# A parallel-mixer decoder layer: the fifth head's division given its natural priority, the seventh head's products with its reciprocals moved to GpSimd

## The chip, the cores and the metric

The kernel runs on one core of a Trainium2 chip. The time is the device time of one execution in microseconds; the time before is the median of three runs. One further execution was taken with the hardware profiler, and all rows below come from it. The engines are called PE (TensorE; PEld is its weight load), DVE (VectorE), ACT (ScalarE), POOL (GpSimd) and SP (SyncE, which here only issues DMAs).

## The reference

One layer over 1024 tokens and 16 meta tokens with 1024 channels. The part around the change is the second of four mixers, causal attention with 8 heads:

```python
z = rms_norm(x) @ w_in                       # one projection for all branches
s = einsum(q, k) masked causally             # per head, 96 wide
o = softmax(s) @ v                           # per head, 64 wide
y_b = (o * silu(mg)) @ w_out_mla             # the heads side by side, gated, projected
m = sum_i sigmoid(g_i) * y_i                 # four mixers; the other three: pooling, two convolutions
x = x + rms_norm(m @ w_o)
```

The softmax is computed as exp(s - max) @ [v, 1]. Its denominator is thus one more row of the product, and the division by it is done afterwards, on the 64 rows of the head's output.

## The kernel before, in words

The kernel has three stages. The first, up to 638 us of the profiled span, is the input projection with the preparation of all branches. The second, from 638 to 838 us, is attention; PE fills its gaps there with the output projections of the three other mixers ("fills", matmuls into the tile ps_y). The third projects the attention's output (ps_u), sums up the mixers and multiplies by w_o.

Every operation is recorded first (`Plan.record`, L325) and put in order by a list scheduler in `Plan.flush` (L364): it walks through an estimated time, and each engine takes of its ready operations the one with the lowest `prio`. An operation's `prio` is its place in the recording minus `lift`; `plan.ahead(n)` (L263) raises `lift` by n, so a negative n puts operations behind some 450 later ones. A DMA's estimated landing has 4500 ns on top of its bytes, and `plan.slow(5000)` adds 5000 (L448, L449). What comes out is a fixed order for each engine; at run time an engine takes its instructions in that order and waits at semaphores. All instructions therefore carry L362, the line that issues them, in the profile, and are told apart by their tiles.

Attention runs over units (h, c): 8 heads, numbered from 0, by two halves of 512 tokens (`attend`, L1507). A unit works through tiles of 128 keys: scores on PE into ps_s (five banks), a mask added by DVE on the diagonal (maskT), exp on ACT to p, a rounded copy on ACT and a residual on POOL (pt; this "split" gives two terms of reduced precision for one of full precision), and the products with v on PE into the one bank ps_o. When a unit ends, ACT copies ps_o to ol (L1556); ol has two buffers, one per head. The row maxima of the next unit (mxs, mr, qt; DVE reading ps_s) go on beside it.

The division of a head, for h < 7, is `sums` (L1558) and `head_out` (L1584). Its steps, in order:

1. SP moves the row of denominators from ol into a 32 x 32 tile lc.
2. DVE takes the reciprocal of lc.
3. SP writes lc to DRAM (r), and then reads it back broadcast over 64 rows into rb (a single buffer).
4. For each half c, DVE multiplies ol by rb into op, 64 rows by 512 columns (L1589). The even head of a pair fills rows 0 to 63, the odd head rows 64 to 127.
5. After the odd head, POOL multiplies op by the gate smg, and ACT and POOL split the result into boM, the operand of the last projection.

An ol buffer is free again once both products of step 4 have read it. The last head (h = 7) takes its reciprocals through PE and multiplies from PSUM (`sums_pe`, L1569). A fill (`fills`, L1603) is six matmuls into one of two ps_y banks, followed on DVE by th<-th,ps_y (gate times projection) and m<-m,th (sum; some of them on POOL).

The loop that records all this sets the priority of the division:

```python
with plan.ahead(300 if h == H - 1 else -450):
    if h == H - 1:
        head_out(h, c, sums_pe(h, c))
    elif c:
        for k, rb in enumerate(sums(h)):
            head_out(h, k, rb)
```

Of the kernel before, what the change touches and what calls it, by code (L numbers as in the profile page):

```python
# [41 lines left out]
H = 8  # L42
# [429 lines left out]
def trunk_kernel(ctx, tc, a):  # L472
    nc = tc.nc
    plan = Plan(nc)
    PE, ACT, DVE, POOL, SP = (plan.engine(e) for e in ("PE", "ACT", "DVE", "POOL", "SP"))
# [7 lines left out]
    def ld(out, in_):  # L483
        SP.dma_start(f(out) if out.dtype == F32R else out, f(in_) if in_.dtype == F32R else in_)
# [10 lines left out]
    def mul(eng, out, x, y):  # L495
        eng.tensor_tensor(out, x, y, op=ALU.mult)

    def split(hi, lo, src, eng=None):
        copy(hi, src)
        sub(eng or POOL, lo, src, f(hi))  # L500
# [937 lines left out]
    def load_q(h, c):  # L1438
        qt[h, c] = qk.tile([NA, 2, 512], F32R, tag="q", bufs=3, name="qt")
        ld(qt[h, c][:QK].rearrange("p s n -> p (s n)"), q_dram[c][h].rearrange("p s n -> p (s n)"))  # L1440
        if h < FIRST:
            ld(f(qt[h, c])[QK:NA, 0], top_dram[:, c].rearrange("r a n -> r (a n)"))
# [18 lines left out]
    def load_k(h, n0, n1):  # L1461
        e = h % 2
        ld(kt[e][:64, :, n0:n1], k_dram[h // 2][64 * e:64 * (e + 1), :, n0:n1])

    def load_kv(h):
        e, k_, v_ = h % 2, kt[h % 2], vt[h % 2]
        k_ = k_[:, :, :L]
        if h < 2:
            k_rows(k_, h, lambda x: x)
        else:  # L1470
            load_k(h, CUT, L)
        if h == 1:
            return
        load_v(h)

    def load_v(h):
        v_ = vt[h % 2]
        v = v_dram[h // 4][h % 4]
        e = v[:NM, 1:9].rearrange("p (c j) d -> p c j d", j=4)[:, :, 3]
        for r, w in ((0, slice(0, P)), (32, slice(0, P)), (64, slice(P, 192))):  # L1480
            ld(vs[h % 2][r:r + NM, :, :w.stop - w.start], e[:, :, w])
        ld(v_[:, 0:8].rearrange("p j c -> p (j c)"), v[:, 0:8].rearrange("p j c -> p (j c)"))
# [22 lines left out]
    ol = {}  # L1505
# [52 lines left out]
    def sums(h):  # L1558

        lc = at.tile([32, 32], F32, tag="lc", bufs=2, name="lc")  # L1560
        rb = at.tile([64, 2, 512], F32, tag="rb", name="rb")
        with plan.slow(5000):
            ld(lc, ol[h][64:65].rearrange("p j (a n) -> p (j a) n", n=32))
            DVE.reciprocal(lc, lc)
            ld(r_dram[h].rearrange("(p n) -> p n", n=32), lc)
            ld(rb.rearrange("p j n -> p (j n)"), r_dram[h].partition_broadcast(64))
        return rb[:, 0], rb[:, 1]

    def sums_pe(h, c):  # L1569

        pc = bank("s")[:, :256].rearrange("p (j n) -> p j n", n=64)
        for j in range(4):
            PE.transpose(pc[:, j].in_order(), ol[h][64:, c, P * j:P * (j + 1)], ident[64:, 64:])
        lc = at.tile([P, 4], F32, tag="lcp", bufs=2, name="lcp")
        with plan.late(700):
            DVE.reciprocal(lc, pc[:, :, 0])
        rb = bank("s")[:64]
        for j in range(4):
            PE.transpose(rb[:, P * j:P * (j + 1)], lc[:, j:j + 1].to_broadcast([P, 64]), ident)
        return rb  # L1580

    op, smg = {}, {}

    def head_out(h, c, rb):  # L1584

        e = h % 2
        if e == 0:
            op[c] = at.tile([P, 512], F32, tag=f"op{c}", name="op")
        mul(DVE, op[c][64 * e:64 * (e + 1), :], ol[h][:64, c], rb)  # L1589
        if e:  # L1590
            mul(POOL, op[c], op[c], smg[h][:, 512 * c:512 * (c + 1)])
            b = boM[c][h // 2]
            split(b[:, 0], b[:, 1], op[c])
# [50 lines left out]
    def refill():  # L1644
        count["u"] += 1
        while count["f"] < min(48, 48 * count["u"] / (NUNIT - 2)):

            with plan.ahead(-400):
                next(fill, None)
            count["f"] += 1  # L1650
# [9 lines left out]
    def lead_to(i, n=0):  # L1660

        while lead["i"] <= min(i, len(seq) - 1) or lead["steps"] < n:
            if next(steps, "end") == "end":
                lead["steps"] = math.inf
            lead["steps"] += 1
# [5 lines left out]
    for i, (h, c) in enumerate(seq):  # L1671
        with plan.behind() if i else nullcontext():
            if i + 2 < len(seq):
                load_q(*seq[i + 2])
            if c == 0 and h + 1 < H:
                load_kv(h + 1)
                if i == 0:
                    with plan.behind():
                        load_v(1)
            if h % 2 and c == int(h < H - 1):  # L1680
                smg[h] = at.tile([P, NT], F32, tag="smg", name="smg")
                ld(smg[h], z_dram[f"mg{h // 2}"])
        for j, _ in enumerate(attend(h, c)):
            if c and j == 4 and h + 2 < H:
                load_k(h + 2, 0, CUT)
            units += 1
            lead_to(-1, min(5 + units * 10 / 14, 5 * (i + 3)))
            refill()
        lead_to(i + 1)

        with plan.ahead(300 if h == H - 1 else -450):
            if h == H - 1:
                head_out(h, c, sums_pe(h, c))
            elif c:
                for k, rb in enumerate(sums(h)):
                    head_out(h, k, rb)
# [247 lines left out]
```

## Time and profile before

| | us |
|---|---|
| median of 3 runs (lowest, highest) | 969.65 (969.29, 969.93) |
| profiled execution, whole time | 968.91 |
| profiled execution, span of its instructions | 967.1 |
| stage 1, 0 to 638: PE busy | 632.59 |
| stage 2, 638 to 838: PE, DVE, ACT, POOL busy | 197.89, 159.01, 115.04, 137.32 |
| stage 3, 838 to 967.1: PE busy | 119.96 |
| granted PE clock, mean | 0.997 |

The span runs from the first to the last instruction of the profiled execution; its whole time is 1.81 us longer. A row of a timeline in this document reads: start in us, duration in us (of several merged instructions where x is above 1), engine, line, operation, output tile <- input tiles, shapes, count, and in brackets how long the engine had been idle just before and what released it. A row of waits reads: engine, tile and line that waited <- what it waited for: us in total, times, longest. A PE that is busy is not one at its peak, since matmuls are pipelined and their ends are modelled. The time recorded for a POOL instruction is rough.

### The profile page before, as it was taken

Reading aid. Unit: us, or ns where it says so; the run is one execution under the profiler, and the core shown is the slowest. Engines: PE = TensorE matmul, PEld = TensorE weight load, DVE = VectorE, ACT = ScalarE, POOL = GpSimd, SP = SyncE. Lnnn points to the kernel's source line nnn. Section 1 sums busy time; section 2 is a strip of 40 time slices with the busy share of each in tenths; the row PEclk is TensorE's granted clock in tenths of the full one; section 3 lists DMA queues with packets and bytes.
Section 4 is the critical chain, followed back from the end, with each engine's and each line's share of the span. In section 5 each row is a group of like instructions: output and inputs, shape, how many; then the busy total and the mean of one; then the engine's idle time right before and its main releaser. Section 6 shows DMA issues by size and latency. Waiting matters only on the chain.

```text
span 967.1 us, 15247 instructions
## 1 busy us (share of the span) xinstructions
PE 950.4 (98%) x5003; PEld 808.9 (84%) x5003; DVE 696.0 (72%) x1113; ACT 449.1 (46%) x914; POOL 678.0 (70%) x628
## 2 busy tenths in 40 slices
PE   8999999999999999999999999999999999999996
PEld 7999899889888887888888878888888788788885
DVE  5856959988779855544536768346778889799757
ACT  7743233444344455554444344366555555225622
POOL 5957555666576787896679679655567786647955
PEclk9999999999999999999999999999999999999998
DMA  8145566668787687787655688699899664783633
GB/s 258 45 126 144 167 198 213 216 196 270 231 265 255 205 248 214 220 255 216 195 168 169 205 268 276 208 318 262 272 221 297 175 187 132 272 267 95 211 113 142
DMA packets 136330, 203.03 MB, mean 210 GB/s; under 512 B 19672, under 2 KB 83159, under 8 KB 135483
## 3 DMA queue, kind: packets, MB, share of 16 engines
q1 hardware_dynamic: 127274, 185.28, 63.3%
q10 hardware_dynamic: 8656, 15.74, 4.4%
q0 software_dynamic: 320, 1.05, 0.3%
q8 instruction: 39, 0.64, 0.3%
q14 instruction: 41, 0.33, 0.1%
HBM read 129.11 MB, written 72.88 MB: 209 GB/s over the span
## 4 chain that ended last, share of the span: by engine, by line
PE 90%; POOL 3%; DVE 2%; issue 2%; ACT 1%; DMA 1%; DVEq 0%; SPq 0%; POOLq 0%; ACTq 0%
PE ps_pa L362 16%; PE ps_pb L362 16%; PE ps_pc L362 15%; PE ps_o L362 9%; PE ps_y L362 8%; PE ps_s L362 8%; PE ps_pd L362 7%; PE ps_u L362 7%; PE ps_x L362 5%; POOL S L362 1%; POOL lsq L362 1%; ACT junk L362 1%; DVE c L362 0%; DMA lacc<-acc 0%; POOL u L362 0%
## 5 line engine op out<-in xcount | busy, mean ns | idle before, releaser
L362 PE MATMUL ps_pb<-T,S 128*128 128x512 f32 (+2 forms) x792 | 172.0, 359 | 0.0
L362 PE MATMUL ps_pa<-B,A 128*128 128x512 f32 (+2 forms) x792 | 171.7, 360 | 0.0
L362 POOL TENSOR_TENSOR A<-raw,A 128x512 fp32r<-128x512 f32 x84 | 114.3, 1368 | 61.3 <-ACT A L362 47.7
L362 PEld LDWEIGHTS ps_pb<-T,S 128*128 128x128 f32 x792 | 134.3, 189 | 22.4 <-issue 1.2
L362 PEld LDWEIGHTS ps_pa<-B,A 128*128 128x128 f32 x792 | 134.4, 188 | 22.3 <-issue 1.0
L362 POOL TENSOR_TENSOR S<-ss,S 128x512 fp32r<-128x512 f32 x84 | 116.0, 1393 | 51.8 <-ACT S L362 51.7
L362 POOL TENSOR_TENSOR pt<-p,pt 128x512 fp32r<-128x512 f32 (+1 forms) x96 | 102.8, 1094 | 52.5 <-PE ps_s L362 32.6
L362 DVE TENSOR_TENSOR u<-ps_pb,u 128x512 f32<-128x512 f32 (+2 forms) x66 | 40.3, 610 | 87.4 <-PE ps_pb L362 84.3
L362 DVE SCALAR_TENSOR_TENSOR ps_w<-conv,par,ps_w 128x512 f32<-128x512 f32 x116 | 87.1, 751 | 2.3
L362 PE MATMUL ps_y<-bo,whl 128*128 128x512 f32 x288 | 85.7, 403 | 0.9 <-DVE th L362 0.9
L362 PE MATMUL ps_pc<-B,S 128*128 128x512 f32 (+1 forms) x396 | 85.8, 358 | 0.0
L362 ACT ACTIVATE S<-ss 128x512 fp32r<-128x512 f32 x84 | 50.4, 627 | 74.5 <-DVE ss L362 43.7
L362 PE MATMUL ps_pd<-T,A 128*128 128x512 f32 (+2 forms) x396 | 84.9, 359 | 0.0
L362 PE MATMUL ps_pc<-T,S 128*128 128x512 f32 (+1 forms) x396 | 84.4, 359 | 0.0
L362 ACT ACTIVATE p<-ps_s 128x512 f32<-128x512 f32 (+4 forms) x112 | 49.7, 444 | 60.3 <-PE ps_s L362 29.2
L362 PEld LDWEIGHTS ps_pc<-T,S 128*128 128x128 f32 x396 | 66.8, 188 | 11.2 <-issue 0.7
L362 PEld LDWEIGHTS ps_pd<-T,A 128*128 128x128 f32 x396 | 67.1, 189 | 10.7
L362 PEld LDWEIGHTS ps_pc<-B,S 128*128 128x128 f32 x396 | 66.4, 189 | 10.2
L362 PE MATMUL ps_o<-pt,vt 128*128 128x512 f32 (+7 forms) x288 | 68.7, 346 | 0.2 <-ACT ol L362 0.2
L362 PE MATMUL ps_s<-qt,kt 100*128 100x512 f32 (+4 forms) x336 | 67.8, 324 | 0.0
L362 PEld LDWEIGHTS ps_s<-qt,kt 100*128 100x128 f32 (+1 forms) x336 | 54.1, 176 | 10.3 <-DVE qt L362 0.6
L362 ACT ACTIVATE A<-raw 128x512 fp32r<-128x512 f32 x84 | 52.0, 626 | 22.3 <-PE ps_pd L362 9.7
(281 smaller groups left out, 1890.4 us busy)
## 6 DMA issues: line engine op xcount, KB each, us to landing
raw<-in_w_in_dram SPq DMA_DIRECT2D x52, 512.0 KB
th<-th SPq DMA_DIRECT2D x32, 512.0 KB
th<-z ACTq DMA_DIRECT2D x60, 256.0 KB
v<-vhl SPq DMA_DIRECT2D x16, 384.0 KB
qt<-q SPq DMA_DIRECT2D x16, 384.0 KB
vt<-v SPq DMA_DIRECT2D x8, 768.0 KB
bo<-bo SPq DMA_DIRECT2D x6, 1024.0 KB
w_out_mla<-whl SPq DMA_DIRECT2D x16, 256.0 KB
```

What stands on the lines that cost most here:

```text
L362: getattr(self.handle[o["eng"]], o["op"])(*map(real, o["args"]), **{k: real(v) for k, v in o["kw"].items()})
```

## The change

Two conditions are added. In `head_out`, the two products ol x rb of h = 6 are issued on POOL and no longer on DVE; their operands and results stay. In the unit loop, all steps of the division of h = 4 are recorded with no lift, where they had a lift of -450. The other heads keep their engine and their priority. As the scheduler orders everything anew, other instructions can change places too.

```diff
@@ head_out @@
         e = h % 2
         if e == 0:
             op[c] = at.tile([P, 512], F32, tag=f"op{c}", name="op")
-        mul(DVE, op[c][64 * e:64 * (e + 1), :], ol[h][:64, c], rb)
+        mul(POOL if h == H - 2 else DVE, op[c][64 * e:64 * (e + 1), :], ol[h][:64, c], rb)
         if e:
             mul(POOL, op[c], op[c], smg[h][:, 512 * c:512 * (c + 1)])
@@ the unit loop @@
-        with plan.ahead(300 if h == H - 1 else -450):
+        with plan.ahead(300 if h == H - 1 else 0 if h == 4 else -450):
             if h == H - 1:
                 head_out(h, c, sums_pe(h, c))
```

## The prediction

> **What bounds the kernel now.** I read first the page's busy shares, then the busy time by stage, the waits of TensorE (PE) in the attention stage, and last the instructions of each engine, in order of time, around the two places that the edits touch.
>
> ```profile
> PE 950.4 (98%) x5003; PEld 808.9 (84%) x5003; DVE 696.0 (72%) x1113; ACT 449.1 (46%) x914; POOL 678.0 (70%) x628
> ```
> ```profile
> 638.00:838.00 200.00, 197.89 (x1059) 164.07 (x1058) 159.01 (x357) 115.04 (x264) 137.32 (x139) 1.00 0.80 232
> ```
> ```profile
> PE ps_s L362 <- ACT p L362: 1.0, 1, 1.0
> PE ps_y L362 <- DVE th L362: 0.9, 1, 0.9
> PE ps_o L362 <- ACT ol L362: 0.2, 1, 0.2
> ```
>
> The stage row gives start and end, length, then busy us (and instructions) of PE, PEld, DVE, ACT, POOL. PE is busy 197.89 of 200 us of attention: both edits lie in a stage with only 2.1 us of recorded PE idleness, and that total is these three waits, 1.0 + 0.9 + 0.2. An edit that takes no matmul away can win about that much here, and can lose more.
>
> The waits of 1.0 and 0.2 belong to the products of the fourth head (heads are counted from 0 in the code, so this is h = 3), which no edit touches:
>
> ```profile
> 767.02 2.68 DVE L362 TENSOR_TENSOR op<-ol,rb 64x512 f32<-64x512 f32 x2
> ...
> 769.74 0.42 PE L362 MATMUL ps_s<-kt,qt 96*128 96x328 f32 x1 [0.95 <-ACT p L362]
> 770.38 3.26 PE L362 MATMUL ps_o<-pt,vt 128*128 128x512 f32 x13 [0.22 <-ACT ol L362]
> ```
>
> The wait of 0.9 stands at the end of the stage, just behind the products of the seventh head (h = 6):
>
> ```profile
> 831.46 0.69 DVE L362 TENSOR_TENSOR m<-m,th 128x512 f32<-128x512 f32 x1
> 832.31 0.69 DVE L362 SCALAR_TENSOR_TENSOR th<-th,ps_y 128x512 f32<-128x512 f32 x1 [0.16 <-PE ps_y L362]
> 833.03 0.69 DVE L362 TENSOR_TENSOR m<-m,th 128x512 f32<-128x512 f32 x1
> 833.75 0.68 DVE L362 TENSOR_TENSOR op<-ol,ps_s 64x512 f32<-64x512 f32 x1
> 834.47 1.29 DVE L362 TENSOR_TENSOR op<-ol,rb 64x512 f32<-64x512 f32 x2
> 835.68 0.67 DVE L362 SCALAR_TENSOR_TENSOR th<-th,ps_y 128x512 f32<-128x512 f32 x1
> 836.39 1.05 DVE L362 TENSOR_TENSOR m<-m,th 128x512 f32<-128x512 f32 x1
> ```
> ```profile
> 836.41 1.67 PE L362 MATMUL ps_y<-bo,whl 128*128 128x512 f32 x6 [0.91 <-DVE th L362]
> ```
>
> VectorE (DVE) runs without a gap here. The pair op<-ol,rb at 834.47 is the h = 6 pair; behind it in DVE's queue stands the th that empties the PSUM bank for which PE waits 0.91 us.
>
> **Edit 1: the h = 6 products go to GpSimd (POOL).** It removes 1.29 us of DVE work ahead of the th of 835.68. It adds two instructions to POOL, whose row at that time is:
>
> ```profile
> 828.93 1.34 POOL L362 TENSOR_TENSOR boM<-op,boM 128x512 fp32r<-128x512 f32 x1 [0.51 <-ACT boM L362]
> 835.23 3.36 POOL L362 TENSOR_TENSOR op<-op,smg 128x512 f32<-128x512 f32 x2 [4.96 <-DVE op L362]
> ```
> ```profile
> L362 POOL TENSOR_TENSOR boM<-op,boM 128x512 fp32r<-128x512 f32 x6 | 7.8, 1302 | 0.6 <-ACT boM L362 0.5
> L362 POOL TENSOR_TENSOR op<-op,smg 128x512 f32<-128x512 f32 x8 | 12.4, 1563 | 5.0 <-DVE op L362 5.0
> ```
>
> POOL has no product of 64 rows, so I bound one by its instructions over 128 rows of the same 512 columns: 1.30 to 1.56 us. The lower end is nearer (the gap is otherwise quiet), so the two take 2.6 us. POOL stands idle for 4.96 us, 830.27 to 835.23, waiting for this very product; the pair fits, and the gates op<-op,smg behind it come no later. What would bite if that cover were gone is told under the rivals.
>
> The price lies on DVE. Its sums m<-m,th take 0.69 us while POOL idles (831.46, 833.03) and 1.05 while POOL works (836.39, inside the row of 835.23). With POOL now busy from 830.3 on, I charge both earlier sums 0.36 us. So the th at 835.68 moves by -1.29 + 2 x 0.36 = -0.57, and PE's wait shrinks from 0.91 to 0.34. Bounds: no charge at all gives -0.91 (PE has nothing more to win there); if each of the two sums waited out a whole POOL instruction, 2 x 1.30, the th comes 1.31 us later and PE loses that much. I take -0.57, by the rows of the same sum in the same place.
>
> A rule speaks against this edit. The Trainium skill, page "SBUF — State Buffer", section "Who interferes with whom", says that a VectorE instruction with two SBUF inputs and a GpSimd instruction that reads SBUF contend for a port pair that is held for the whole instruction, so that the later one stands still. The sums' 0.69 and 1.05 us agree with a wait of that kind that is only partly served out; by the rule's worst case the term would be +1.31 in place of -0.57, which is the rival "lock" below.
>
> Behind the stage, PE's first products ps_u want the last boM. With the pair done early, the gates are held by op<-ol,ps_s of h = 7 (833.75, done 834.43) and no longer by the pair's end near 835.76. So boM comes over a microsecond earlier, while PE comes at most 0.91 earlier; no new wait arises, and as none of PE's three waits lies there, none goes. I count 0.
>
> **Edit 2: the h = 4 division at its natural place.** The priority of all of its steps rises by 450 places: the DMA of the sums, the reciprocal, two more DMAs on SP, and two products. Their places now:
>
> ```profile
> 754.15 0.56 SPq L362 DMA_DIRECT2D lc<-ol  x1
> ...
> 766.99 0.38 SPq L362 DMA_DIRECT2D r<-lc  x1
> 771.41 0.46 SPq L362 DMA_DIRECT2D rb<-r  x1
> ...
> 822.27 0.46 SPq L362 DMA_DIRECT2D rb<-r  x1
> ```
> ```profile
> 789.54 1.70 DVE L362 TENSOR_TENSOR op<-ol,rb 64x512 f32<-64x512 f32 x1
> 791.55 1.38 DVE L362 TENSOR_TENSOR op<-ol,rb 64x512 f32<-64x512 f32 x1
> ```
>
> The three DMAs (754.15, 766.99, 771.41) are short issues of 0.38 to 0.56 us on SP; rb has a single buffer, which the h = 3 products hold until 769.70, so rb cannot come much before 771.41. Only the products can move far: from 789.54 to no earlier than about 775.8 (771.41 plus the 4.42 us that lie between r<-lc and the rb<-r behind it, as nearest row for a landing). The planner charges such a transfer some 10 us (4.5 + 5 and the bytes), so I place them near 782. Moved: 1.70 + 1.38 = 3.08 us of DVE from behind to ahead of the row maxima, mask adds and bank evacuations of 782 to 789. Queued behind them are PE's bank turnover and the qt rows of the next unit. PE shows no gap in this stretch (columns as in the stage row):
>
> ```profile
> 780.00:790.00 10.00, 10.00 (x53) 8.11 (x52) 8.82 (x21) 5.00 (x14) 7.35 (x9) 1.00 0.67 204
> ```
>
> Nothing can be won at the spot itself. What hides the move is DVE's 1.18 idle us of 780 to 790 and PE's filler matmuls. If that does not do, the row of its kind is h = 3, where such a pair cost 0.95 + 0.22 = 1.17 us; of the six pairs of h = 0 to 5 it is the only one with a PE wait beside it, since the stage has no PE wait but the three above. So 0 to +1.17; I take 0, by five of six.
>
> It also frees the ol buffer early. Now the copy of h = 6 waits for it, while PE works fillers:
>
> ```profile
> 792.97 0.60 ACT L362 ACTIVATE ol<-ps_o 128x512 f32<-128x512 f32 x1 [0.20 <-DVE op L362]
> ```
> ```profile
> 785.71 0.24 PE L362 MATMUL ps_o<-pz,vs 80*128 80x16 f32 x1
> ...
> 785.90 1.36 PE L362 MATMUL ps_y<-bo,whl 128*128 128x512 f32 x5
> 791.65 1.32 PE L362 MATMUL ps_y<-bo,whl 128*128 128x512 f32 x5
> 792.94 1.09 PE L362 MATMUL ps_y<-bo,whl 128*128 128x512 f32 x4
> ```
> ```profile
> 838.08 43.57 PE ps_u L362 x192
> ```
>
> The bank is complete at 785.95 and is copied out at 792.97. With ol free the copy moves some 6 us forward, and up to 14 fillers (at 43.57 / 192 = 0.227 us, 3.2 us) are put off. The number of matmuls stays, so PE's sum stays; the late fillers need DVE, 0.67 + 0.69 to 1.05 us for each six, against 6 x 0.227 = 1.36 of PE. That is 0 to 0.36 us per six, at most 0.8 for fourteen, under a DVE gap of 3.58 us ahead of 825.41:
>
> ```profile
> 825.41 0.69 DVE L362 SCALAR_TENSOR_TENSOR th<-th,ps_y 128x512 f32<-128x512 f32 x1 [3.58 <-PE ps_y L362]
> ```
>
> I take 0. **Sum:** -0.57 + 0 + 0 = -0.57. The profiled execution took 968.91 us (span 967.1 and 1.81 around it), so about 968.3; it lies 0.74 below the median of 969.65, to which I add the same step: 969.1.
>
> **The rivals.**
>
> *Stall at the new place.* The h = 4 pair makes PE wait as h = 3 does: -0.57 + 1.17 = +0.60, 970.3. For it: DVE is 88% busy there. Against: five of six pairs.
>
> *Lock.* Each sum beside a POOL product waits it out: +1.31, 971.0. For it: op<-ol,rb takes 1.70 and 1.38 beside a busy POOL and 0.65 without. Against: the sum at 836.39, beside POOL, takes only 1.05. With the stall as well it is +2.48, 972.1.
>
> *Slower: POOL's queue.* The planner's landing time for rb of h = 6 is a guess. If the products stand ahead of head 7's last residual splits, POOL waits in order:
>
> ```profile
> 821.23 3.94 POOL L362 TENSOR_TENSOR pt<-p,pt 128x512 fp32r<-128x512 f32 x4
> ```
> ```profile
> 836.92 0.63 ACT L362 ACTIVATE boM<-op 128x512 fp32r<-128x512 f32 x1 [7.42 <-POOL op L362]
> ```
>
> rb is issued at 822.27 and, by the 4.42 us above, there at 826.7; the splits would start at 826.7 + 2.6 = 829.3, 8.1 us late. The unit behind them, and with it op<-ol,ps_s of 833.75, ends 8.1 us later, at 842.5; gate, rounding and residual (1.30 + 0.63 + 1.30) give boM at 845.8, where PE asks for it at 837.92 + 22 x 0.227 = 842.9. PE loses 2.9 us, net +2.3: 972.0. It decides from a delay of the splits of 5.2 us on. Against: the planner's 10 us are more than the 4.42, so it would place the pair behind the splits.
>
> *Faster: both waits go.* Everything is ordered anew from the DMA of 754.15 on, so the waits at 769 may vanish with the one at 836: -2.1, 967.6. Against: the h = 3 products that cause them keep their priority.
>
> *No move.* The planner finds no earlier place for the h = 4 pair; edit 1 works alone: 969.1, as forecast.
>
> **How the numbers follow.** Forecast, with no move: 0.47. Stall 0.10, lock 0.06, both 0.05, POOL's queue 0.12, both waits gone 0.20. A difference under 0.2% (1.94 us) cannot be told from no change here. Faster, under 967.7: 0.20. Slower, over 971.6: 0.12 + 0.05 = 0.17. Within: 0.63. The range goes from 967.2, which takes in most of the fast case, to 971.2, which takes in stall and lock and leaves the 0.17 out.
>
> **What would show it.** Right: no op<-ol,rb on DVE between 825 and 838 and two on POOL near 1.3 us each ahead of the last gates; the wait ps_y <- DVE th at the end at 0.3 us, with the sums there near 1.05; the h = 4 pair near 782 and the copy of h = 6 near 786; PE waits of the stage near 1.5 us. Wrong: a PE wait of 1 us or more between 775 and 800, a POOL gap in front of its op<-ol,rb while pt is waiting, DVE sums near 2 us, or a stage that ends beyond 838.5 or before 836.5.

## The result and the profile after

| | before | after |
|---|---|---|
| median of 22 runs each, on the same chips, us | 969.93 | 968.57 |
| lowest to highest | 968.72 to 972.6 | 967.86 to 970.89 |
| ratio, with its 95% interval | | 0.9987 [0.9981, 0.9993] |
| profiled execution: span | 967.1 | 967.1 |
| attention in it, first ps_s to first ps_u | 638.11 to 837.92 = 199.81 | 639.39 to 838.38 = 198.99 |

By the ratio the changed kernel is faster by 0.13%, which is 1.26 us (0.68 to 1.84); the two medians differ by 1.36. That is inside the 0.2% that the prediction called no change, though this many runs can tell it from nothing. The forecast of 969.1 is 0.5 us too high.

The two profiled executions have the same span, because the one of after lost 1.28 us before attention began (639.39 against 638.11). PE has the same order of work up to there in both kernels, all 3407 of its recorded matmuls. The chain of waits of after has, near its start, a longer load of the input, `x<-in_x_dram`, of 7.56 us from 2.13, where the one of before has 3.47 us from 1.19. I therefore compare attention by itself, where the changed kernel needs 0.82 us less.

First the busy shares of the page of after, then its row for the 200 us of attention (columns as in the prediction), then its PE waits in the stage:

```profile
PE 952.0 (98%) x5003; PEld 809.9 (84%) x5003; DVE 692.5 (72%) x1111; ACT 449.4 (46%) x914; POOL 680.3 (70%) x630
```
```profile
638.00:838.00 200.00, 199.07 (x1062) 164.77 (x1061) 157.01 (x354) 115.26 (x264) 141.11 (x143) 1.00 0.79 230
```
```profile
PE ps_s L362 <- DVE mxs L362: 0.6, 1, 0.6
PE ps_y L362 <- DVE th L362: 0.2, 1, 0.2
```

Two instructions have gone from DVE (1113 to 1111) to POOL (628 to 630). PE is idle less. Of the three waits of before, the one on th has shrunk from 0.9 to 0.2, as the prediction had it. The other two, 1.0 and 0.2 near 769, are gone, and a wait of 0.6 on a row maximum, mxs, is new. The forecast counted on neither of these two, though two of its rivals had named them.

**The end of attention.** DVE, PE and POOL of after, in order of time, at the place of edit 1:

```profile
832.64 1.06 DVE L362 TENSOR_TENSOR m<-m,th 128x512 f32<-128x512 f32 x1
833.62 0.67 DVE L362 SCALAR_TENSOR_TENSOR th<-th,ps_y 128x512 f32<-128x512 f32 x1
834.33 1.07 DVE L362 TENSOR_TENSOR m<-m,th 128x512 f32<-128x512 f32 x1
835.43 0.68 DVE L362 TENSOR_TENSOR op<-ol,ps_s 64x512 f32<-64x512 f32 x1
836.14 0.69 DVE L362 SCALAR_TENSOR_TENSOR th<-th,ps_y 128x512 f32<-128x512 f32 x1
836.86 2.72 DVE L362 TENSOR_TENSOR m<-m,th 128x512 f32<-128x512 f32 x1
```
```profile
836.88 1.66 PE L362 MATMUL ps_y<-bo,whl 128*128 128x512 f32 x6 [0.24 <-DVE th L362]
```
```profile
831.41 1.74 POOL L362 TENSOR_TENSOR op<-ol,rb 64x512 f32<-64x512 f32 x1
833.23 1.62 POOL L362 TENSOR_TENSOR op<-op,smg 128x512 f32<-128x512 f32 x1
834.81 1.74 POOL L362 TENSOR_TENSOR op<-ol,rb 64x512 f32<-64x512 f32 x1
836.51 1.27 POOL L362 TENSOR_TENSOR boM<-op,boM 128x512 fp32r<-128x512 f32 x1
837.75 1.28 POOL L362 TENSOR_TENSOR op<-op,smg 128x512 f32<-128x512 f32 x1
```

The pair op<-ol,rb is on POOL. The two sums ahead of the last th (the one that starts at 836.14, for which PE waits) take 1.06 and 1.07 us where they took 0.69, and PE waits 0.24 us.

**The place of edit 2.** Here three rows of the before, which the prediction had not needed, stand first, two of DVE and one of PE:

```profile
764.76 0.33 DVE L362 RECIPROCAL lc<-lc 32x32 f32<-32x32 f32 x1
...
770.65 0.69 DVE L362 SCALAR_TENSOR_TENSOR th<-th,ps_y 128x512 f32<-128x512 f32 x1
```
```profile
766.78 0.66 PE L362 MATMUL ps_y<-bo,whl 128*128 128x512 f32 x2
```

The same stretch of DVE in after, and behind it the new place of the h = 4 pair:

```profile
762.87 0.33 DVE L362 RECIPROCAL lc<-lc 32x32 f32<-32x32 f32 x1
...
766.05 0.69 DVE L362 SCALAR_TENSOR_TENSOR th<-th,ps_y 128x512 f32<-128x512 f32 x1
...
767.59 1.63 DVE L362 TENSOR_TENSOR op<-ol,rb 64x512 f32<-64x512 f32 x1
...
769.54 1.38 DVE L362 TENSOR_TENSOR op<-ol,rb 64x512 f32<-64x512 f32 x1
...
781.31 1.09 DVE L362 TENSOR_TENSOR op<-ol,rb 64x512 f32<-64x512 f32 x1
783.59 1.76 DVE L362 TENSOR_TENSOR op<-ol,rb 64x512 f32<-64x512 f32 x1 [1.19 <-POOL boM L362]
785.28 0.93 DVE L362 TENSOR_REDUCE mxs<-ps_s 128x1 f32<-128x348 f32 x2
```

PE of after at both places:

```profile
763.74 0.62 PE L362 MATMUL ps_y<-bo,whl 128*128 128x512 f32 x2
...
769.87 1.63 PE L362 MATMUL ps_y<-bo,whl 128*128 128x512 f32 x6
771.34 0.32 PE L362 MATMUL ps_s<-kt,qt 96*128 96x328 f32 x1
...
785.84 0.39 PE L362 MATMUL ps_s<-kt,qt 96*128 96x272 f32 x1 [0.56 <-DVE mxs L362]
```

In before, the h = 3 pair (767.02) stands ahead of a th at 770.65. In after, a th stands at 766.05, ahead of that pair; six fills run at 769.87, and PE doesn't wait.

Counting the rows shows that these are the same th and the same bank. The fills take the two ps_y banks in turn, six matmuls each, and all 288 of these matmuls and all 48 reads of their banks are in both traces. The six at 769.87 are the 29th group and need the bank that the 27th read empties. That read is the th of 766.05 in after, 126.7 us from the start of attention, and the th of 770.65 in before, at 132.5 us, so that there the 29th group could not have filled the gap. The 27th group is also complete sooner. Its sixth matmul is the second in the row of 763.74 in after; in before it is the first in the row of 766.78, behind a block of scores. That sixth matmul is the first place at which the two orders of PE differ in attention, as the reciprocal of h = 4 is on DVE.

At the new place of the h = 4 pair the row maximum at 785.28 comes behind it, and PE waits 0.56 us for it.

**Where PE loses time, by stretch.** The table is worked out from the traces. For each PE matmul of attention I take the time from its start to the start of the next, less the shortest such spacing (fastest tenth over the runs) of a matmul of its shape. That excess is summed over stretches counted in us from the start of attention: 130 to 140 is 768 to 778 in the span of before, 140 to 150 is 778 to 788, the last is 828 to 838. The work itself is 184.9 us in every run. The first column changes by 0.9 us between two executions of one kernel (after and h1), so it is left out of the last column.

```
                               0-60  60-130 130-140 140-150 150-190 190-end   60-end
before                          4.08   3.65   1.94   0.89   2.26   2.13      10.87
after                           4.07   3.60   0.55   2.22   2.31   1.39      10.07
h1_changed_again                4.98   3.52   0.62   2.24   2.34   1.35      10.07
e1_pool_only                    4.26   3.59   1.93   0.90   2.28   1.43      10.13
f2_frozen_pool                  4.12   3.58   1.92   0.93   2.26   1.42      10.11
f1_frozen_no_division           4.61   3.57   1.94   0.90   2.26   1.03       9.70
e2_h4_only                      4.33   3.60   0.55   2.22   2.33   2.05      10.75
e3_h4_sums_only                 4.50   3.58   0.55   1.74   3.28   2.10      11.25
e4_h4_products_only             4.07   3.60   1.93   1.94   2.33   2.05      11.85
e5_no_h6_products               5.06   3.71   2.04   0.93   2.27   2.33      11.28
g1_early_sums_late_products     4.26   3.59   0.50   0.68   3.45   0.87       9.09
h2_late_products_again          4.49   3.60   0.55   0.66   3.47   0.86       9.14
g2_late_products_6us            4.09   3.61   0.54   0.76   3.43   1.44       9.78
```

Changed against before, the rows of the table say: -1.39 near 769, +1.33 near 785, -0.74 at the end, and -0.80 over all from 60 on. Both profiles of the changed kernel give the same 10.07. Two orders were profiled twice (after and h1, g1 and h2), and each repeats within 0.1 us in every column but the first. So these columns tell differences of a few tenths apart where the times, with intervals near 0.1%, cannot.

### The profile page after: what moved, and what is told of

It reads as the page before. It is cut to its first block, busy times and chain, and to the rows that moved or that the text cites. A ratio compares the mean times of both kernels' runs of the same rounds, so it can differ in the third digit from the quotient of the medians.

```text
span 967.1 us, 15246 instructions
## 1 busy us (share of the span) xinstructions
PE 952.0 (98%) x5003; PEld 809.9 (84%) x5003; DVE 692.5 (72%) x1111; ACT 449.4 (46%) x914; POOL 680.3 (70%) x630
## 3 DMA queue, kind: packets, MB, share of 16 engines
q0 software_dynamic: 320, 1.05, 0.3%
## 4 chain that ended last, share of the span: by engine, by line
PE 88%; POOL 4%; DVE 3%; issue 2%; ACT 1%; DMA 1%; SPq 0%; DVEq 0%; ACTq 0%; POOLq 0%
PE ps_pa L362 16%; PE ps_pb L362 16%; PE ps_pc L362 15%; PE ps_o L362 9%; PE ps_u L362 7%; PE ps_s L362 7%; PE ps_pd L362 7%; PE ps_y L362 6%; PE ps_x L362 5%; POOL S L362 1%; DMA x<-in_x_dram 1%; POOL lsq L362 1%; DVE th L362 1%; POOL pt L362 0%; ACT junk L362 0%
```

## The experiments

Each kernel was timed in 11 or 12 runs beside the kernel before on the same chip.

**The two edits apart.** `e1_pool_only` has the first changed line alone, `e2_h4_only` the second.

```diff
-        mul(DVE, op[c][64 * e:64 * (e + 1), :], ol[h][:64, c], rb)
+        mul(POOL if h == H - 2 else DVE, op[c][64 * e:64 * (e + 1), :], ol[h][:64, c], rb)
```

> The products of h = 6 on POOL, the division of h = 4 with its old priority. Theory A (the forecast's: edit 1 carries the gain, through DVE's queue at the end): 0.5 to 0.8 us faster than before (ratio 0.9992 to 0.9995), the PE wait ps_y <- DVE th at the end falls from 0.91 to 0.2 to 0.4 us, the waits of 0.95 and 0.22 us near 769 stay. Theory B (the gain comes from the new order that edit 2 brings): no difference (ratio 0.9997 to 1.0003).

```diff
-        with plan.ahead(300 if h == H - 1 else -450):
+        with plan.ahead(300 if h == H - 1 else 0 if h == 4 else -450):
```

> The division of h = 4 at lift 0, the products of h = 6 on DVE as before. Theory A: no difference (ratio 0.9997 to 1.0003), the end's wait of 0.9 us stays. Theory B: the waits of 1.17 us near 769 go and a wait of 0.56 us for mxs near 786 comes, as in the profile of the changed kernel, so 0.6 us faster (ratio 0.9993 to 0.9995).

Measured: e1 968.82 against 969.38, ratio 0.9992 [0.9983, 1.0001]; e2 969.97 against 969.38, 1.0004 [0.9995, 1.0013]. The PE waits of e1 in attention, then those of e2:

```profile
PE ps_s L362 <- ACT p L362: 0.9, 1, 0.9
PE ps_y L362 <- DVE th L362: 0.3, 1, 0.3
PE ps_o L362 <- ACT ol L362: 0.2, 1, 0.2
```
```profile
PE ps_y L362 <- DVE th L362: 0.9, 1, 0.9
PE ps_s L362 <- DVE mxs L362: 0.5, 1, 0.5
```

Edit 1 alone keeps the waits near 769 and shrinks the one at the end: last stretch 2.13 to 1.43. Edit 2 alone removes the waits near 769, makes the one on mxs, and leaves the end as it was: -1.39 and +1.33 in the two stretches, -0.12 from 60 on. By the table the edits add up: -0.74 and -0.12 against -0.80 together. Edit 1 carries the gain in attention and edit 2 nets about nothing, by two changes that cancel: e2's waits went as theory B had it, and its time about as theory A had it. By the times alone this isn't shown, since both intervals hold 1.

**Which part of edit 2 does which.** `e3_h4_sums_only` lifts only the steps up to rb; the products keep -450. `e4_h4_products_only` lifts only the products. Both leave edit 1 out.

```diff
@@ e3, on top of edit 2 @@
-            for k, rb in enumerate(sums(h)):
-                head_out(h, k, rb)
+            with plan.ahead(0):
+                rbs = sums(h)
+            with plan.ahead(-450 if h == 4 else 0):
+                for k, rb in enumerate(rbs):
+                    head_out(h, k, rb)
@@ e4, on top of before @@
+            rbs = sums(h)
+            with plan.ahead(450 if h == 4 else 0):
+                for k, rb in enumerate(rbs):
+                    head_out(h, k, rb)
```

> Of the division of h = 4 only the DMAs and the reciprocal get lift 0, its products keep -450; the products of h = 6 stay on DVE. If the waits near 769 went because the reciprocal and its DMAs come earlier (theory B1), they are gone here too, and the wait for mxs near 786 does not come: 1.0 to 1.2 us faster (0.9988 to 0.9990). If they went because of the moved products (B2), they are still here: no difference.

> Of the division of h = 4 only the two products get lift 0; the DMAs and the reciprocal keep -450; the products of h = 6 stay on DVE. Theory C (the early reciprocal is what fills the gap of h = 3: it lets the emptying of a ps_y bank slip ahead of the h = 3 products): the waits of 1.17 us near 769 stay here. The pair at its new place costs what it costs with all of edit 2: a wait for mxs of 0.5 us and some 0.6 us around it. So 0.5 to 1.2 us slower (ratio 1.0005 to 1.0012). If the waits near 769 go here as well, C is wrong.

Measured: e3 970.51 against 969.38, 1.0007 [0.9999, 1.0016]; e4 970.87 against 969.42, 1.0011 [1.0002, 1.0019]. DVE of e3 and then its PE:

```profile
762.52 0.33 DVE L362 RECIPROCAL lc<-lc 32x32 f32<-32x32 f32 x1
...
765.71 0.69 DVE L362 SCALAR_TENSOR_TENSOR th<-th,ps_y 128x512 f32<-128x512 f32 x1
...
781.86 3.16 DVE L362 TENSOR_TENSOR op<-ol,rb 64x512 f32<-64x512 f32 x2
```
```profile
769.53 1.63 PE L362 MATMUL ps_y<-bo,whl 128*128 128x512 f32 x6
...
785.83 0.39 PE L362 MATMUL ps_s<-kt,qt 96*128 96x264 f32 x1 [0.56 <-DVE mxs L362]
```

PE waits of e4:

```profile
PE ps_s L362 <- ACT p L362: 1.0, 1, 1.0
PE ps_y L362 <- DVE th L362: 0.9, 1, 0.9
PE ps_o L362 <- POOL pt L362: 0.7, 1, 0.7
PE ps_o L362 <- ACT ol L362: 0.2, 1, 0.2
```

With the early sums alone the waits near 769 go, and with the early products alone they stay (stretch 130 to 140: 0.55 and 1.93). So it is the early sums that clear 769. In e3 as in after, the reciprocal stands about 3 us earlier, counted from the start of attention (123.9 and 123.5 us, 126.7 in before), the same th follows ahead of the h = 3 pair, and the same six fills run where PE waited. Why the scheduler then takes the sixth fill and that th sooner is not on record, and no run moved them alone.

The products went near 782 in all three kernels, in e3 even at lift -450. e3 has them back to back, without the 1.19 us that the second product of after waited for POOL, and PE waits the same 0.56 us. So that wait comes from where the pair stands, ahead of a row maximum, and not from the product that was held up. The whole excess there is another matter: it is 2.22 in after and e2, but 1.74 in e3 and 1.94 in e4, where the pair also runs without a gap; so up to 0.5 of the 1.33 may belong to the held product. In e4 the wait at this place is also another one, 0.7 on POOL's pt. For e3 the mxs wait was expected not to come and a gain of 1.0 to 1.2 us was; both failed, since the lower priority did not keep the pair back, and another 1.02 was lost between 150 and 190. By the table, each half done alone costs time (11.25 and 11.85 against 10.87); by the times, only e4's interval lies above 1.

**What could edit 1 win at most?** `e5_no_h6_products` leaves the h = 6 products out, so that the seventh head is missing from the result, and lets the scheduler order the rest.

```diff
-        mul(DVE, op[c][64 * e:64 * (e + 1), :], ol[h][:64, c], rb)
+        if h == H - 2:
+            POOL.memset(op[c][:64], 0.0)
+        else:
+            mul(DVE, op[c][64 * e:64 * (e + 1), :], ol[h][:64, c], rb)
```

> The two products of h = 6 are left out: POOL fills their 64 rows with zeros in their place, so the seventh head's output is missing from the result. This is the ceiling of edit 1: neither engine pays for them. Theory A: the end's wait goes wholly, 0.9 us faster (ratio 0.9990 to 0.9992), and no more, since PE has nothing else to win there. If more goes (1.5 us or above), the products also cost something that PE's records do not show as waiting.

Measured: 969.4 against 969.38, 1.0 [0.9991, 1.0009]. DVE has less to do, and yet the excess from 60 on is 11.28 instead of 10.87, and PE waits 0.7 us on th. That is not the gain of 0.9 us that was expected. The scheduler had built another order, so this run says nothing on what the products cost. The next two keep the order of before, instruction by instruction, and change only the engine on which the two products of h = 6 are issued: `f1_frozen_no_division` lets ACT copy ol into op in their place, which leaves the seventh head undivided; `f2_frozen_pool` issues the products on POOL. The line that issues each operation (`Plan.issue`) is changed to go by these entries and is not shown.

```diff
@@ f1, behind the mul of head_out @@
+        if h == H - 2:
+            plan.ops[-1].update(issue=("ACT", "activation"),
+                                args=(op[c][:64], ol[h][:64, c], AF.Copy), kw={})
@@ f2, at the same place @@
+        if h == H - 2:
+            plan.ops[-1]["issue_on"] = "POOL"
```

> The order of every engine is that of the kernel before, kept by planning the old products; only when the two products of h = 6 are issued, ACT copies ol to op in their place, so the seventh head's output is not divided by its sums. Neither DVE nor POOL pays for them: the ceiling of edit 1 with nothing reordered. Theory A (DVE's queue at the end holds PE for 0.91 us): attention gets 0.9 us shorter (ratio 0.9990 to 0.9992) and the wait ps_y <- DVE th goes. If leaving the products out costs time here too, as it did where the planner reordered (attention 1.4 us longer in that profile), A is wrong; A says that there it was the new order.

> The order of the kernel before on every engine, but the two products of h = 6 are issued on POOL, at the place that they have in that order (behind boM of the pair before, ahead of the gates). Theory A: as with edit 1 alone, attention 0.5 to 0.7 us shorter (ratio 0.9992 to 0.9995), since the gain is the work taken from DVE and not an order that the planner finds. Rival (order): under 0.2 us.

Measured: f1 968.96 against 969.42, 0.9993 [0.9984, 1.0001]; f2 969.17 against 969.42, 0.9994 [0.9986, 1.0003]. The PE waits of f1 (whose issuing line is L363), then DVE of f2 at the end, and its POOL:

```profile
PE ps_s L363 <- ACT p L363: 0.9, 1, 0.9
PE ps_s L363 <- DMA qt<-q: 0.3, 1, 0.3
PE ps_o L363 <- ACT ol L363: 0.2, 1, 0.2
```
```profile
835.23 0.69 DVE L362 SCALAR_TENSOR_TENSOR th<-th,ps_y 128x512 f32<-128x512 f32 x1
835.95 3.99 DVE L362 TENSOR_TENSOR m<-m,th 128x512 f32<-128x512 f32 x1
```
```profile
830.50 3.42 POOL L362 TENSOR_TENSOR op<-ol,rb 64x512 f32<-64x512 f32 x2
833.90 2.98 POOL L362 TENSOR_TENSOR op<-op,smg 128x512 f32<-128x512 f32 x2
836.84 2.55 POOL L362 TENSOR_TENSOR boM<-op,boM 128x512 fp32r<-128x512 f32 x2
```

f1 has no wait on th at the end, and its last stretch falls by 1.10 to 1.03: that is the ceiling. (Its wait on a load of qt lies in the first column.) f2, with the order of before, falls by 0.71 to 1.42, as e1 with its own order does. So edit 1 wins by the work it takes off DVE ahead of the last th, not by a new order, and gets about two thirds of what there was.

**Early sums and late products.** If the early sums win 1.39 us near 769 and the pair costs 1.33 near 785, the pair should be kept behind the row maxima. `g1_early_sums_late_products` is the changed kernel, with the scheduler told that rb of h = 4 lands 8 us later; `g2_late_products_6us` says 6 us.

```diff
@@ sums, the load of rb, on top of the changed kernel @@
-            ld(rb.rearrange("p j n -> p (j n)"), r_dram[h].partition_broadcast(64))
+            with plan.slow(8000 if h == 4 else 0):
+                ld(rb.rearrange("p j n -> p (j n)"), r_dram[h].partition_broadcast(64))
```

> The changed kernel, but the planner is told that rb of h = 4 lands 8 us later than it assumed, which puts the two products behind the qt rows of the next unit; the early reciprocal stays, and the products of h = 6 stay on POOL. Theory C: the waits near 769 stay away and the wait for mxs near 786 is gone too; with the 0.6 of edit 1 attention is 1.6 to 2.0 us shorter than before (ratio 0.9980 to 0.9985), 0.8 to 1.2 us shorter than in the changed kernel. Rival (some wait always comes up in a new order): as the changed kernel, 0.9987 to 0.9992.

> The changed kernel itself, beside the two below on one chip. By the first comparison, 0.9981 to 0.9993 of the time before.

> Early sums, late products (8 us) once more, to be compared with the changed kernel on the same chip. Theory C: 0.8 us under it, as their attention stages stood (198.21 against 198.99 us); 0.9978 to 0.9986 of the time before.

> As the kernel with late products, but with 6 us in place of 8: the h = 4 products stand right behind the qt rows and the next sum on DVE, and the fifth to eighth heads' later order is nearer that of the changed kernel. Theory C: the waits near 769 and 786 are both away, attention 1.6 to 2.2 us shorter than before (0.9978 to 0.9984). If the pair still makes PE wait at this place (0.5 us or more between 780 and 795), it is as fast as the changed kernel.

Here h1 is the changed kernel once more and h2 is g1 once more, on one chip with g2. Measured: g1 967.8 against 969.42, 0.9986 [0.9976, 0.9996]; and against 969.57, h1 968.67, 0.9989 [0.998, 0.9998]; h2 967.96, 0.9989 [0.9978, 1.0]; g2 968.12, 0.9985 [0.9976, 0.9994]. DVE of g1, and its PE, which has one wait in all of attention:

```profile
784.69 0.68 DVE L362 TENSOR_TENSOR qt<-ps_s,ident 4x512 fp32r<-4x512 f32 x1
...
788.11 2.38 DVE L362 TENSOR_TENSOR op<-ol,rb 64x512 f32<-64x512 f32 x2
```
```profile
768.75 1.63 PE L362 MATMUL ps_y<-bo,whl 128*128 128x512 f32 x6
...
824.89 0.93 PE L362 MATMUL ps_o<-pt,vt 128*128 128x512 f32 x3 [0.37 <-POOL pt L362]
836.28 4.02 PE L362 MATMUL ps_u<-boM,whl 128*128 128x512 f32 x17
```

The pair now stands behind the qt row, the excess of 140 to 150 falls from 2.22 to 0.68, that of 130 to 140 stays low, and attention takes 198.21 us. Of the 1.54 won there, 1.14 is lost again between 150 and 190 (2.31 to 3.45), 0.37 of it in the wait on pt shown above, and another 0.52 is won at the end; both repeat in h2. How these two follow stays open. By the medians the version is 0.71 us faster than the changed kernel on the same chip (h2, h1) and the excess from 60 on is over 0.9 us smaller in both executions of each. In time, the intervals of h1 and h2 overlap, so that it beats the changed kernel is shown by the traces and not by the times. The ratio of h2 lies outside the 0.9978 to 0.9986 that was expected, though its interval reaches across them. g2 wins less than was expected (1.6 to 2.2 us of attention): by its excess it is 1.09 under before, and waits on mxs and th, 0.3 and 0.6 us in all, are left in it.

## Why the prediction was right, and where it was not

**The forecast and its range.** 969.1 was forecast, 968.57 measured; a step of -0.57 was forecast, -1.26 measured, with an interval from -0.68 to -1.84. Attention accounts for -0.8. Behind the stage the prediction counted 0. There the profile of after is 0.44 us shorter, 128.69 us against 129.14, and nearly all of it lies in the tail behind the start of the last matmul, 8.98 and 9.37 us; PE's own way from the first ps_u to that matmul is 119.71 and 119.76. The tail ranges from 8.89 to 9.83 us over the thirteen profiles, and it goes with the order: 8.97 in h1, 9.28 in both g1 and h2, and 9.34 in f2, which has the order of before. So the edits probably reach it through the new order of DVE, ACT and POOL behind attention. Which part of that order shortens it stays open.

**Edit 1: right in mechanism, terms mis-sized.** The forecast was a th earlier by 0.57, a wait of 0.34 left of 0.91. Measured are a wait of 0.24, and -0.70 to -0.74 in the last stretch, in e1, f2 and the changed kernel alike. In f2, with the order held, the th starts 0.71 us earlier, counted from the start of attention. Both sums did slow as charged, to 1.06 and 1.07 from 0.69, but the first of them delayed what follows by only 0.14 us: from its start to that of the next th is 0.99 us in f2 and 0.85 in before, where DVE stood idle for 0.16 us ahead of that th. This gap is in the prediction's own row of 832.31; "VectorE (DVE) runs without a gap here" overlooked it. The POOL product, put at 1.3 us by the quiet POOL rows, took 1.74; PE has no recorded wait behind it. Too low was the bound's use of the wait: 0.91 of recorded wait was taken as all that could be won, while f1 shows 1.10. The row of PE waits doesn't hold all the time that PE loses.

On the rule of the Trainium skill, page "SBUF — State Buffer", section "Who interferes with whom": its worst case of +1.31 did not come about ahead of the last th. Just behind that th the next sum took 2.72 us in after and 3.99 in f2, longer than any one POOL instruction there; PE has no recorded wait behind it.

**"The waits of 1.0 and 0.2 belong to the products of the fourth head (...), which no edit touches": wrong, and the step that failed.** They belonged to the order around these products. Lifting the sums of h = 4 by 450 moved its reciprocal, 0.33 us long, some 3 us ahead, and in the new order a th slipped in front of the h = 3 pair: it starts 126.7 us into attention, where the reciprocal had stood in before. Six fills then ran where PE had waited: -1.39. The prediction named this outcome as the rival "both waits go" (0.20) and argued against it with that same step. Of its -2.1, 1.39 and 0.74 did come, and another wait took back 1.33.

**"Nothing can be won at the spot itself ... 0 to +1.17; I take 0, by five of six": right in the sum by luck, wrong in both its terms.** Nothing makes the -1.39 and the +1.33 alike; that they cancel is chance. The pair moved to 781.31, near the 782 forecast, and the stall of the kind of h = 3 came, at +1.33 slightly over its bound. So the mechanism of the rival "stall at the new place" (0.10) is what happened at the new place, and only the gain near 769 hides it. The prediction had named the row maxima that the pair would stand ahead of, the first of which behind it starts at 785.28, but it went by the count of pairs, which does not ask what stands behind this one. The copy of h = 6 stands at 788.20 instead of 792.97. Counted from the start of attention it moved 6.05 us, the "some 6 us" of the prediction, though not to 786, for attention began later and the copy's own bank came 0.9 us later in it:

```profile
788.20 0.60 ACT L362 ACTIVATE ol<-ps_o 128x512 f32<-128x512 f32 x1 [1.27 <-PE ps_o L362]
```

It no longer waits for DVE. The 14 fills put off cost at most little: 150 to 190 is 2.26 and 2.31.

**The other rivals.** POOL's queue did not block: the first POOL product stands at 831.41, behind the splits, as argued. The order did change, so "no move" is out.

## What to carry to other kernels

Under a scheduler that orders everything anew, an edit's place of effect is not where its instructions are: ask what a step that moves lets slip past, back to the step's first instruction, and not only what it delays. To learn what an instruction costs, take it out with the order held fixed; taken out with the order free, it measured another order (e5 against f1). And when a small net change is read, read it by stretch first: here two terms of 1.3 us cancelled, and keeping the one without the other was the better version.

## What the runs showed of the hardware

A DVE sum, m<-m,th over 128x512, took 0.68 to 0.69 us wherever no POOL instruction ran beside it (152 sums in the thirteen profiles). Where POOL did run it took anything from 0.68 to 3.99 us (368 sums); the two ahead of the last th in after took 1.06 and 1.07. In two places shown above it took far longer: 2.72 us from 836.86 in after, where POOL ran 1.27 us from 836.51 and 1.28 us from 837.75 without a gap; and 3.99 us from 835.95 in f2, where POOL ran its products without a gap from 833.90 to 839.39. In both, the sum ended 0.55 us after POOL's row did (839.58 against 839.03, 839.94 against 839.39). So a sum that meets a row of POOL instructions without gaps can wait out several and not just the one it met. It need not: in before POOL runs without a gap from 835.23 to 841.99, the second half of it in this row,

```profile
838.55 3.44 POOL L362 TENSOR_TENSOR boM<-op,boM 128x512 fp32r<-128x512 f32 x2
```

and the three sums inside that time took 1.05, 1.07 and 1.07 us. What decides between the two is open, and that both engines want the same port is not shown by these rows alone. What such a meeting costs POOL is not known: its product over 64 rows took 1.74 us beside DVE, and no run has one with DVE quiet.
